# A gated feed-forward block on one core: two more block pairs by seven products, an order of its own for the up projection, and weights laid out as tiles

## The chip, the core and the metric

The kernel runs on one core of one Trainium2 chip. A core has a matrix engine (TensorE, PE in the profile), VectorE (DVE), ScalarE (ACT), GpSimd (POOL) and a sync engine (SP) that issues transfers (DMA). The metric is the device time of one execution in microseconds.

## The reference

One encoder layer on 256 tokens of width D = 2048, in float32, with inputs x, p and the layer's weights:

```python
hn = rmsnorm(x, mix_norm_pre)
z, xbc, dt_raw, u = split(hn @ w_in)
y = concat(ssd_mixer(z, xbc, dt_raw, ...), pool_mixer(u, pool_w, pool_scale))
h = x + rmsnorm(y @ w_out, mix_norm_post)
hn = rmsnorm(h, ffn_norm_pre)
gate, val = split(hn @ w_ffn_up)                      # 2048 -> 2 x 5632
gate = dwconv_centred(gate, ffn_conv_w, ffn_conv_b)   # 3 taps over the tokens, a channel at a time
ff = (gelu(gate) * val) @ w_ffn_down                  # 5632 -> 2048
h = h + rmsnorm(ff, ffn_norm_post)
g = sigmoid(rmsnorm(h, ple_norm_pre) @ w_ple_gate)
out = h + rmsnorm(g * (p @ w_ple), ple_norm_post)
```

Here rmsnorm(v, g) is v divided by the root of its mean square (plus 1e-6) along the channels, times g. `ssd_mixer` is a two-way state-space scan with 16 heads, `pool_mixer` a set of four centred means over windows of 2, 4, 8 and 16 tokens, each followed by a linear map.

## The kernel before

**Numbers in two parts.** Every matmul operand is split into a high part (a cast on ACT to the matmul's reduced float format) and a low part (a subtraction on DVE: the number less its high part). A product takes three matmuls: high by high, high by low and low by high. `split` does that for weights, in pieces of at most 128x1024, into two rings of five buffers each (`whi`, `wlo`); the pieces come from `raw` pages (three buffers of 128x2048), which SP fills by DMA. Further buffers are `page` (13 of 128x2048, for everything long-lived), `mid` (three of 128x1024), `hs` (two of 128x1024, for split hidden values) and eight PSUM banks.

**Stages, in order of time.** The input projection (dtu, xbc, z), the mixers, the output projection (wo), the per-layer embedding's first half (ple0), **up** (11 slabs of 512 hidden channels; each slab has two gate blocks ga and two value blocks va of 64 matmuls), **down** (dn, two halves of 1024 output columns), the second half of the embedding (ple1), the gate (gt), and the end.

**Up.** `feature_pairs` multiplies a block's weights with the normalised input, 16 matmuls for each piece of 128x1024; the norm itself is applied afterwards. `total` adds the two halves of the PSUM result into SBUF (an ACT copy and a DVE add of 128x256, twice for each block). For gates a DVE multiply by the row norm `rfb` follows, then `conv` (three taps for a channel group, on DVE), the gelu on ACT, and once for each slab a 128x1024 DVE multiply by `rfb`, which gives the values their norm (the gelu's result is later multiplied with the values). The product of gelu and values is stored in the six `hid` pages.

**Down.** `token_major` runs over 22 pairs of contraction blocks of 128. A slow pair takes 24 matmuls of 128x512 for a half. A fast pair goes through `seven_products`: a scheme like Strassen's with seven block products for eight, 21 matmuls. It needs sums of weight blocks (`block_sums`, `add_blocks`) and sums of hidden blocks (`pair_sums`, `hid_sums`). `dn_fast` lists the fast pairs, 12 of 22 in either half. The sums of weights for all fast pairs of down and four of gt are made while up runs: `block_sums` fetches a page (dnb, gtb), adds on DVE (L235 to L237) and stores the result to DRAM (dns, gts) through SP; 26 are stored and the last two, for down's first fast pairs, are held in their pages. Sums of hidden blocks are made on DVE (four 128x128 operations, a cast, a 128x512 subtraction) when a pair comes up; four of the twelve are kept in two pages (`dn_keep`) for the second half. `get_hid` casts and subtracts two hidden blocks at a time into an hs buffer.

**What sets the order.** A scheduler of the tile framework orders each engine's instructions by data, by free buffers and by place in the program; it can take work ahead of its place. `tc.issue_after(i)` makes what is issued under it come after instruction i. An engine then works strictly in the order that results. `aside` pops one job of the list `work` after each u step of up. `ready` holds pieces that were split ahead, `at` jobs at a given pair of the second half: `back` (loads the residual h from DRAM into pages hb) at 13 and `first_gate` at 16, which makes the first gate pair's parts from a page gtf, the low part by a copy with negative sign and an accumulating transfer from POOL's queue.

Of the kernel before, what the change touches and what calls it, by code (L numbers as in the profile page):

```python
# [11 lines left out]
F32 = mybir.dt.float32  # L12
F32R = mybir.dt.float32r
AF = mybir.ActivationFunctionType
ALU = mybir.AluOpType

P = 128
# [6 lines left out]
NF = DFF // P  # L24
DPLE = 256
# [26 lines left out]
def build(nc, a, out):  # L52
    x = a["x"][0]
    w_in, w_out, w_up = a["w_in"][0], a["w_out"][0], a["w_ffn_up"][0]
    w_down, w_gate, w_ple = a["w_ffn_down"][0], a["w_ple_gate"][0], a["w_ple"][0]
    out = out[0]

    with tile.TileContext(nc) as tc, \
# [37 lines left out]
        c_dt = DSSD + 1536  # L96
        r0 = wp.tile([P, 2048], F32, tag="raw", bufs=3, name="dtur0")
        for n in range(2):
            first = ins(nc.scalar.dma_start(r0[:, n * 352:(n + 1) * 352],
                                            w_in[:P, c_dt + n * 352:c_dt + (n + 1) * 352]))  # L100
# [55 lines left out]
        def raw(name, src, a_, b_):  # L156
            r = wp.tile([P, 2048], F32, tag="raw", bufs=3, name=name)
            if src is None:
                return r
            last["dma"] = load(r[:, :a_ * b_].rearrange("p (a b) -> p a b", a=a_), src, True)  # L160
            return r
# [33 lines left out]

        def aside():

            for job in (work.pop(0) if work else ()):
                job()
# [8 lines left out]
        def block_sums(name, w, c0, k, held):  # L208


            pg = []

            def fetch():
                r = page(f"{name}b{c0}_{k}")
                pg.append(r)
                load(r.rearrange("p (k c) -> p k c", k=2),
                     w[k * P:(k + 2) * P, c0:c0 + 1024].rearrange("(k p) c -> p k c", p=P))
# [12 lines left out]
            return [fetch], [], [add], [store]  # L230

        def add_blocks(r):

            v = r.rearrange("p (b c) -> p b c", b=4)
            nc.vector.tensor_add(v[:, 0:2], v[:, 0:2], v[:, 1::2])  # L235
            nc.vector.tensor_add(v[:, 3], v[:, 3], v[:, 0])
            nc.vector.tensor_add(v[:, 2], v[:, 2], v[:, 3])  # L237

        def seven_products(name, stage, w, k0, c0, a_, acc, alt, start, stop):
# [3 lines left out]
            if (stage, c0, k0) in sums_:  # L243
                r = raw(f"{name}r", None, 0, 0)
                last["dma"] = load(r[:, 512:1536], w[(k0 + 1) * P:(k0 + 2) * P, c0:c0 + 1024], True)
                last["dma"] = load(r[:, :512], w[k0 * P:(k0 + 1) * P, c0:c0 + 512], True)
# [4 lines left out]
                b11 = split(f"{name}a", r[:, :512], 512)  # L251
                b2 = split(f"{name}b", r[:, 512:1536], 1024)
            else:
                r = t = raw(f"{name}r", w[k0 * P:(k0 + 2) * P, c0:c0 + 1024]
                            .rearrange("(k p) c -> p k c", p=P), 2, 1024)
                b11 = split(f"{name}a", r[:, :512], 512)
                b2 = split(f"{name}b", r[:, 1024:], 1024)
                add_blocks(r)
            t13 = split(f"{name}c", t[:, :1024], 1024)
            t42 = split(f"{name}d", t[:, 1024:], 1024)  # L260
            for x, (wh, wl), c, o, own in (
                    ("a11", b11, 0, alt[0], True), ("a12", b2, 0, acc[0][0], False), ("s4", b2, 512, acc[0][1], False),
                    ("s1", t13, 0, alt[1], True), ("s3", t13, 512, alt[2], True), ("a22", t42, 0, acc[1][0], False),
                    ("s2", t42, 512, alt[3], True)):
# [26 lines left out]
        def token_major(name, w, c0, ks, get, acc, tail=1, fast=(), alt=None, sums=None, at=()):  # L291
# [3 lines left out]
            for u in range(nu):  # L295
# [3 lines left out]
                if u in fast:  # L299
                    if u == fast[0]:  # L300
# [3 lines left out]
                r = None if f"{name}{k0}_0" in ready else raw(f"{name}r{k0}", w[k0 * P:(k0 + 2) * P, c0:c0 + 1024]  # L304
                                                               .rearrange("(k p) c -> p k c", p=P), 2, 1024)
# [8 lines left out]
                for t, (o, c), (k, wh, wl), q in order:  # L314
                    xh, xl = (v[:, t * P:(t + 1) * P] for v in get(k))
                    xx, ww = ((xh, wh), (xh, wl), (xl, wh))[q]
                    mm(o, xx, ww[:, c:c + o.shape[-1]], k == ks[0] and q == 0, k == ks[-1] and q == 2)
# [3 lines left out]
                aside()  # L321

        def feature_major(name, w, c0, get, acc):

            for u in range(4):
                r = raw(f"{name}r{u}", w[u * 512:(u + 1) * 512, c0:c0 + 512]
                        .rearrange("(k p) c -> p k c", p=P), 4, 512)
# [12 lines left out]
        def feature_pairs(name, w, c0, get, acc):  # L340


            for u in range(2):
                r = raw(f"{name}r{u}", w[u * 1024:(u + 1) * 1024, c0:c0 + 256]
                        .rearrange("(k p) c -> p k c", p=P), 8, 256)
                for j in range(2):
                    wh, wl = split(f"{name}{u}_{j}", r[:, j * 1024:(j + 1) * 1024], 1024)
                    for kk in range(4):
                        k = 8 * u + 4 * j + kk
                        for f in range(2):  # L350
                            s = slice(kk * 256 + f * P, kk * 256 + (f + 1) * P)
                            mm(acc[f], wh[:, s], get.both(k), k == 0, False)
                            mm(acc[f][:, L:], wl[:, s], get(k)[0], False, k == NK - 1)
                aside()
# [88 lines left out]
        for u in range(0, NK, 2):  # L443
            r = [wp.tile([P, 2048], F32, tag="raw", bufs=3, name=f"dtur{u}") if u else r0, page(f"dtur{u + 1}")]
            for j in range(2):
                k = u + j
                if k == 0:
                    last["dma"] = load(r[0][:, 704:1056], w_in[:P, c_dt + 704:c_dt + 1056])
# [3 lines left out]
                for c0, c1 in ((0, 704), (704, 1056)) if k == 1 else ((0, 1056),):  # L452
                    last["dma"] = load(r[j][:, c0:c1], w_in[k * P:(k + 1) * P, c_dt + c0:c_dt + c1])
# [29 lines left out]
        with tc.issue_after(half[0]), tc.issue_after(half[1]):  # L483
# [11 lines left out]
            for a_ in range(4):  # L495
# [17 lines left out]
        load(pmat.rearrange("p (g s t) -> p g s t", g=4, s=2),  # L513
             a["pool_matrix"].rearrange("g (s p) t -> p g s t", p=P))
        poolw = page("poolw")
        load(poolw.rearrange("p (g c d) -> p g c d", g=4, c=2),
             a["pool_w"][0].rearrange("g (c p) d -> p g c d", p=P))
# [122 lines left out]
        def xbc(slab):  # L640
            acc = main(f"xbc{slab}")
            feature_major(f"xb{slab}", w_in, DSSD + slab * 512, hn, acc)
# [88 lines left out]
        token_major("z", w_in, 0, list(range(NK)), hn, zacc)  # L731
# [42 lines left out]
        def pair_sums(name, s, o, a11, a21, a12, a22):  # L774

            s1, s2, s3, s4 = (s[:, i * P:(i + 1) * P] for i in range(4))
# [5 lines left out]
            nc.vector.tensor_sub(o[:, 512:], s[:, :512], o[:, :512].bitcast(F32))  # L782
            return {f"s{i + 1}": (o[:, i * P:(i + 1) * P], o[:, 512 + i * P:512 + (i + 1) * P]) for i in range(4)}
# [22 lines left out]
        def sublayer(name, w, ks, get, gain, h, vnext, panel=Panel, fast=((), ()), sums=None, at=()):  # L806
# [3 lines left out]
            for half in range(2):  # L810
# [6 lines left out]
                for t in range(2):  # L817
                    for n in range(2):
# [4 lines left out]
                        nc.scalar.activation(junk, b, AF.Square, accum_out=q)  # L823
                        nc.vector.tensor_mul(mg[t][:, c], b, gain[:, c])
# [40 lines left out]
        dn_fast, gt_fast, dn_keep = ((2, 3, 5, 7, 8, 10, 12, 13, 15, 16, 18, 19), (2, 3, 5, 7, 8, 10, 12, 13, 15, 16, 18, 19)), ((4, 6), (1, 2)), (3, 8, 13, 18)  # L865
# [7 lines left out]
        hid = []  # L873
        for s in range(DFF // 512):
            sc = mid(f"gr{s}")
            for i in range(2):
                ga = main(f"ga{s}{i}")
                feature_pairs(f"ug{s}{i}", w_up, s * 512 + i * 256, hf, ga)
                o = sc[:, i * 512:(i + 1) * 512]
                total(o, ga)  # L880
                v = o.rearrange("p (f t) -> p f t", f=2)
                nc.vector.tensor_tensor(v, v, rfb.unsqueeze(1).to_broadcast([P, 2, L]), op=ALU.mult)
            cv = conv(f"fc{s}", sc, 3, V_FCW + 4 * s, NF, V_FCB + 4 * s)
            nc.scalar.activation(cv, cv, AF.Gelu_apprx_tanh)
            nc.vector.tensor_tensor(cv.rearrange("p (f t) -> p f t", f=4), cv.rearrange("p (f t) -> p f t", f=4),
                                    rfb.unsqueeze(1).to_broadcast([P, 4, L]), op=ALU.mult)
            for i in range(2):
                va = main(f"va{s}{i}")
                feature_pairs(f"uv{s}{i}", w_up, DFF + s * 512 + i * 256, hf, va)
                c0 = (s % 2) * 1024 + i * 512  # L890
                if len(hid) == s // 2:
                    hid.append(page(f"hid{s // 2}"))
                hd = hid[s // 2][:, c0:c0 + 512]
                total(hd, va)
                nc.vector.tensor_mul(hd, hd, cv[:, i * 512:(i + 1) * 512])
# [3 lines left out]
        def get_hid(k):  # L899
            if k % 2 == 0:  # L900
                t = lp.tile([P, 1024], F32R, tag="hs", bufs=2, name=f"hs{k}")
                src = hid[k // 8][:, (k % 8) * L:(k % 8 + 2) * L]
# [187 lines left out]
```

## Time and profile before

| | us |
|---|---|
| median of 3 runs | 1123.46 (1123.09 to 1123.56) |
| the profiled execution's own time | 1123.46 |
| its span, first to last instruction | 1121.6 |
| front: input projection, mixers, output projection (0 to 296) | 296 |
| up, with ple0 ahead of it (296 to 789.1) | 493 |
| down, half 0 and half 1 (789.1 to 1017) | 228 |
| ple1, gate and end (1017 to 1121.6) | 105 |

The granted TensorE clock was 0.999 of full speed on average. In the profile, lines like L87 are lines of the kernel's source; all matmuls are issued from L87 of `mm`, so they are told apart by the names of their result and operands (ga, va for up, dna, dns, dn0s, dn1s for down, gt for the gate). A row of a group has the line, the engine, the operation, out<-in, the shapes, the count, then busy time in us and the mean of one in ns, then idle time of that engine ahead of them and what released it. A row of a timeline or of the chain begins with the start and the duration in us.

### The profile page before, as it was taken

Reading aid. Unit: us, or ns where it says so; the run is one execution under the profiler, and the core shown is the slowest. Engines: PE = TensorE matmul, PEld = TensorE weight load, DVE = VectorE, ACT = ScalarE, POOL = GpSimd, SP = SyncE. Lnnn points to the kernel's source line nnn. Section 1 sums busy time; section 2 is a strip of 40 time slices with the busy share of each in tenths; the row PEclk is TensorE's granted clock in tenths of the full one; section 3 lists DMA queues with packets and bytes.
Section 4 is the critical chain, followed back from the end, with each engine's and each line's share of the span. In section 5 each row is a group of like instructions: output and inputs, shape, how many; then the busy total and the mean of one; then the engine's idle time right before and its main releaser. Section 6 shows DMA issues by size and latency. Waiting matters only on the chain.

```text
span 1121.6 us, 15747 instructions
## 1 busy us (share of the span) xinstructions
PE 1111.2 (99%) x5975; PEld 957.1 (85%) x5975; DVE 928.0 (83%) x1291; ACT 665.4 (59%) x929; POOL 31.1 (3%) x69
## 2 busy tenths in 40 slices
PE   9999999999999999999999999999999999999997
PEld 9999988888888888888888888888888888888876
DVE  6468897799898877877877768878799999899795
ACT  6848663555764554554545545545677777786673
POOL 0200000100100000000000000000000000001001
PEclk9999999999999999999999999999999999999999
DMA  9853447456799989999999898996969688995673
GB/s 361 312 197 104 162 161 277 151 188 189 252 320 349 316 298 340 303 295 313 341 319 310 289 335 303 313 297 218 321 198 336 219 292 295 381 323 175 231 235 107
DMA packets 145996, 300.87 MB, mean 268 GB/s; under 512 B 5504, under 2 KB 98560, under 8 KB 137856
## 3 DMA queue, kind: packets, MB, share of 16 engines
q1 hardware_dynamic: 145216, 298.19, 78.8%
q0 software_dynamic: 272, 1.05, 0.5%
q8 instruction: 47, 0.77, 0.3%
q10 hardware_dynamic: 432, 0.62, 0.2%
q14 instruction: 29, 0.24, 0.1%
HBM read 268.38 MB, written 31.46 MB: 267 GB/s over the span
## 4 chain that ended last, share of the span: by engine, by line
PE 95%; ACT 2%; DVE 1%; issue 1%; DMA 0%; POOL 0%; SPq 0%; POOLq 0%; ACTq 0%
PE va L87 22%; PE ga L87 21%; PE dna L87 14%; PE woa L87 7%; PE xbc L87 6%; PE gt L87 5%; PE z L87 4%; PE dtu L87 4%; PE dns L87 3%; PE dn0s L87 1%; PE dn1s L87 1%; PE ple L87 1%; PE pw L87 1%; PE yd L87 1%; DMA dtur<-w_in 0%
## 5 line engine op out<-in xcount | busy, mean ns | idle before, releaser
L87 PE MATMUL ga<-wox,ug_0h 128*128 128x512 f32 x352 | 125.5, 395 | 0.0
L87 PE MATMUL ga<-wox,ug_1h 128*128 128x512 f32 x352 | 125.1, 394 | 0.0
L87 PE MATMUL va<-wox,uv_1h 128*128 128x512 f32 x352 | 124.8, 393 | 0.0
L87 PE MATMUL va<-wox,uv_0h 128*128 128x512 f32 x352 | 124.8, 393 | 0.0
L87 PE MATMUL ga<-wox,ug_1l 128*128 128x256 f32 x352 | 99.2, 282 | 0.0
L87 PE MATMUL ga<-wox,ug_0l 128*128 128x256 f32 x352 | 99.1, 282 | 0.0
L87 PE MATMUL va<-wox,uv_1l 128*128 128x256 f32 x352 | 99.1, 281 | 0.0
L87 PE MATMUL va<-wox,uv_0l 128*128 128x256 f32 x352 | 99.1, 281 | 0.0
L87 PEld LDWEIGHTS va<-wox,uv_1h 128*128 128x128 f32 x352 | 66.1, 188 | 15.0
L87 PEld LDWEIGHTS va<-wox,uv_0h 128*128 128x128 f32 x352 | 66.1, 188 | 15.0
L87 PEld LDWEIGHTS ga<-wox,ug_0h 128*128 128x128 f32 x352 | 66.1, 188 | 14.9
L87 PEld LDWEIGHTS ga<-wox,ug_1h 128*128 128x128 f32 x352 | 66.1, 188 | 14.9
L87 PEld LDWEIGHTS ga<-wox,ug_0l 128*128 128x128 f32 x352 | 66.2, 188 | 0.1
L87 PEld LDWEIGHTS ga<-wox,ug_1l 128*128 128x128 f32 x352 | 66.2, 188 | 0.0
L87 PEld LDWEIGHTS va<-wox,uv_1l 128*128 128x128 f32 x352 | 66.2, 188 | 0.0
L87 PEld LDWEIGHTS va<-wox,uv_0l 128*128 128x128 f32 x352 | 66.2, 188 | 0.0
L87 PE MATMUL dna<-dn_0h,hs 128*128 128x512 f32 x160 | 50.1, 393 | 0.0
L87 PE MATMUL dna<-dn_1h,hs 128*128 128x512 f32 x160 | 49.9, 393 | 0.0
L235 DVE TENSOR_TENSOR dnb<-dnb 128x1024 f32<-128x1024 f32 x24 | 29.3, 1222 | 14.0 <-DMA dnb<-w_ffn_down 14.0
L903 ACT CAST hs<-hid 128x512 fp32r<-128x512 f32 x44 | 27.1, 617 | 18.3 <-PE dna L87 18.3
L904 DVE TENSOR_TENSOR hs<-hid,hs 128x512 fp32r<-128x512 f32 x44 | 30.2, 686 | 9.1 <-ACT hs L903 9.0
L428 DVE SCALAR_TENSOR_TENSOR fc<-gr,vt,fc 128x255 f32<-128x255 f32 x88 | 36.8, 479 | 0.1
(1909 smaller groups left out, 3060.3 us busy)
## 6 DMA issues: line engine op xcount, KB each, us to landing
dnb<-w_ffn_down SPq DMA_DIRECT2D x24, 1024.0 KB, 10.3
dns<-dnb SPq DMA_DIRECT2D x22, 1024.0 KB, 6.9
dn0r<-w_ffn_down SPq DMA_DIRECT2D x10, 1024.0 KB, 6.2
dn1r<-w_ffn_down SPq DMA_DIRECT2D x10, 1024.0 KB, 6.9
zr<-w_in SPq DMA_DIRECT2D x8, 1024.0 KB, 5.2
dtur<-w_in SPq DMA_DIRECT2D x14, 528.0 KB, 8.5
wo0r<-w_out SPq DMA_DIRECT2D x7, 1024.0 KB, 5.5
wo1r<-w_out SPq DMA_DIRECT2D x6, 1024.0 KB, 5.7
```

The costliest lines, as they stand in the source:

```text
L87: last["pe"] = ins(nc.tensor.matmul(o, lhsT, rhs, start=start, stop=stop, skip_group_check=True))
L235: nc.vector.tensor_add(v[:, 0:2], v[:, 0:2], v[:, 1::2])
L428: nc.vector.scalar_tensor_tensor(o[:, lo:hi], i[:, lo + d:hi + d], vec(wcol + j * wstep + f), o[:, lo:hi], op0=ALU.mult, op1=ALU.add)
L903: nc.scalar.copy(t[:, :512], src)
L904: nc.vector.tensor_sub(t[:, 512:], src, t[:, :512].bitcast(F32))
```

## The change

1. `dn_fast` has 14 of 22 pairs in either half: 2, 3, 4, 5, 7, 8, 9, 11, 12, 13, 15, 16, 18, 19. There are 32 block sums for 28; the last two, for pairs 2 and 3 of half 0, are held.
2. Up has an order of its own. `in_order` chains all ACT, DVE and SP instructions of up, each engine's in program order. `next_part` splits weight pieces five ahead of their matmuls. The jobs of a block sum stand at fixed pieces: fetch at piece 11·i/2 + 2, add and store three pieces later. `add_blocks` makes four adds of 128x512, and the store is issued from POOL instead of SP.
3. Eight sums of hidden blocks (pairs 2, 3, 5, 8, 11, 13, 16, 19) are made during up in an hs buffer, stored to DRAM from POOL, and loaded by POOL in both halves of down into a `mid` buffer. The pages of `dn_keep` are gone.
4. The values go without the norm; the evictions of down get it as a scale instead (ACT's square with scale=row, DVE's scalar-tensor-tensor for the multiply by the gain).
5. The convolution has its three taps on ACT and two adds of 2x255 on DVE, for each gate block.
6. The host lays out the weights as tiles, so that a partition's row of a transfer is contiguous (8 KB for a page). The first-level loads of a fast pair become one transfer of 6 KB a partition.
7. `seven_products` uses its pieces in the order a, b, d, c, with the products a11, a12, a22, s4, s2, s1, s3.
8. The first gate pair is split by ACT and DVE at pair 11 of half 1; ple1's weights are split ahead; the reload of h stands after the last pair; ple0's result is kept in DRAM and loaded back.
9. `get_hid` issues its cast and subtraction after the last ACT and the last DVE instruction of up.

```diff
 def add_blocks(r):
     v = r.rearrange("p (b c) -> p b c", b=4)
-    nc.vector.tensor_add(v[:, 0:2], v[:, 0:2], v[:, 1::2])
-    nc.vector.tensor_add(v[:, 3], v[:, 3], v[:, 0])
-    nc.vector.tensor_add(v[:, 2], v[:, 2], v[:, 3])
+    for i, j in ((1, 0), (0, 3), (3, 1), (2, 3)):
+        nc.vector.tensor_add(v[:, i], v[:, i], v[:, j])
...
 def store():                                   # of block_sums
     if not held:
         t = dp.tile([P, 2048], F32, ...)
-        load(t, pg[0])
+        nc.gpsimd.dma_start(t, pg[0])
...
+def in_order():
+    block = nc.cur_bb.bb.instructions
+    seen = {i.name for i in block}
+    yield
+    for i in block:
+        if i.name in seen or i.engine not in ORDERED:
+            continue
+        if i.engine in chain:
+            tc.add_manual_dep(i, chain[i.engine].name, ..., reason="in_order")
+        chain[i.engine] = i
...
-nc.scalar.activation(junk, b, AF.Square, accum_out=q)
-nc.vector.tensor_mul(mg[t][:, c], b, gain[:, c])
+nc.scalar.activation(junk, b, AF.Square, scale=row[t], accum_out=q)
+nc.vector.scalar_tensor_tensor(mg[t][:, c], b, row[t], gain[:, c], op0=ALU.mult, op1=ALU.mult)
...
+dn_stored = (2, 3, 5, 8, 11, 13, 16, 19)
-work.extend([] for _ in range(8 * DFF // 512))
+jobs_at = [[] for _ in range(NPIECES)]          # NPIECES = 176
 for i, w_ in enumerate(which[2:] + which[:2]):
-    for j, jobs in enumerate(block_sums(*w_, i >= len(which) - 2)):
-        work[3 * i + 2 + j].extend(jobs)
+    fetch, add, store = block_sums(*w_, i >= len(which) - 2)
+    n = 11 * i // 2 + 2
+    jobs_at[n].append(fetch)
+    jobs_at[n + 3].extend((add, store))
...
+for u in dn_stored:
+    jobs_at[16 * (u // 2) + 4 * (u % 2) + 13].extend(hid_sums_jobs(2 * u))
...
+def gate_conv(s, i):
+    v, c, l = (m[:, i * 512:(i + 1) * 512].rearrange("p (f t) -> p f t", f=2) for m in slab[s])
+    for f in range(2):
+        w = V_FCW + 4 * s + 2 * i + f
+        nc.scalar.activation(c[:, f], v[:, f], AF.Identity, bias=vec(...), scale=vec(w + NF))
+        nc.scalar.activation(l[:, f], v[:, f], AF.Copy, scale=vec(w))
+        nc.scalar.activation(v[:, f], v[:, f], AF.Copy, scale=vec(w + 2 * NF))
+    nc.vector.tensor_add(c[:, :, 1:], c[:, :, 1:], l[:, :, :L - 1])
+    nc.vector.tensor_add(c[:, :, :L - 1], c[:, :, :L - 1], v[:, :, 1:])
...
+with in_order():
+    for _ in range(5):
+        next_part()
+    for n in range(NPIECES):
+        s, v, i = blocks[n // 4]
+        if n % 4 == 0:
+            acc = main(f"{'gv'[v]}a{s}{i}")
+        feature_pairs(n % 4, parts[n], hf, acc)
+        if n % 4 == 3:
+            (value_out if v else gate_out)(s, i, acc)
+        next_part()
+        if n >= 4 and n % 4 < 2 and blocks[n // 4 - 1][1] == 0:
+            (gelu if n % 4 else gate_conv)(blocks[n // 4 - 1][0], blocks[n // 4 - 1][2])
+        for job in jobs_at[n]:
+            job()
+ends = [chain[e] for e in ORDERED[:2]]
...
 def get_hid(k):
     if k % 2 == 0:
         t = lp.tile([P, 1024], F32R, tag="hs", bufs=2, name=f"hs{k}")
-        nc.scalar.copy(t[:, :512], src)
-        nc.vector.tensor_sub(t[:, 512:], src, t[:, :512].bitcast(F32))
+        with tc.issue_after(ends[0]), tc.issue_after(ends[1]):
+            nc.scalar.copy(t[:, :512], hid_part(k))
+            nc.vector.tensor_sub(t[:, 512:], hid_part(k), t[:, :512].bitcast(F32))
...
 def hid_sums(k):
     (h1, l1), (h2, l2) = get_hid(k), get_hid(k + 1)
+    o = mid(f"hd{k}", F32R)
+    if k in kept:
+        nc.gpsimd.dma_start(o.bitcast(F32), kept[k])
+        d = sums_in(o)
+    else:
+        d = hid_sums_of(k, sp.tile([P, 512], F32, tag="junk", bufs=1, name=f"hs{k}"), o)
...
-              fast=dn_fast, sums=hid_sums, at={13: back, 16: first_gate})
+              fast=dn_fast, sums=hid_sums, at={11: first, NF // 2: lambda: (ple_parts(), back())}, row=rf)
```

`value_out` and `gate_out` are `total` followed by the multiply with the gelu's result, or with `rfb`.

More of the change, by code (lines that the diff above doesn't have):

```diff
@@ L24 @@
 NF = DFF // P
+NPIECES = DFF // 32
 DPLE = 256
@@ L154, in split, with raw @@
             return hi, lo
-        def raw(name, src, a_, b_):
+        def raw(name, src=None):
             r = wp.tile([P, 2048], F32, tag="raw", bufs=3, name=name)
-            if src is None:
-                return r
-            last["dma"] = load(r[:, :a_ * b_].rearrange("p (a b) -> p a b", a=a_), src, True)
+            if src is not None:
+                last["dma"] = load(r, src, True)
             return r
@@ L338, in feature_major, with feature_pairs @@
                 aside()
[L340 to L354, printed above, removed]
+        def feature_pairs(n, part, get, acc):
+            wh, wl = part
+            for kk in range(4):
+                k = 4 * n + kk
+                for f in range(2):
+                    s = slice(kk * 256 + f * P, kk * 256 + (f + 1) * P)
+                    mm(acc[f], wh[:, s], get.both(k), k == 0, False)
+                    mm(acc[f][:, L:], wl[:, s], get(k)[0], False, k == NK - 1)
         def total(o, acc):
@@ L804, in __call__, with sublayer @@
                             a22=(h2[:, P:], l2[:, P:]))
-        def sublayer(name, w, ks, get, gain, h, vnext, panel=Panel, fast=((), ()), sums=None, at=()):
+        def sublayer(name, w, ks, get, gain, h, vnext, panel=Panel, fast=((), ()), sums=None, at=(), row=None):
             mg = [page(f"{name}m{t}") for t in range(2)]
@@ new lines, in build, with hid_part, hid_sums_of, hid_sums_jobs @@
+            fetch, add, store = block_sums(*w_, i >= len(which) - 2)
+            n = 11 * i // 2 + 2
+            jobs_at[n].append(fetch)
+            jobs_at[n + 3].extend((add, store))
+        hid, kept = [], {}
+        def hid_part(k):
+            return hid[k // 8][:, (k % 8) * L:(k % 8 + 2) * L]
+        def hid_sums_of(k, s, o):
+            return pair_sums(f"he{k}", s, o, *(hid_part(k)[:, i * P:(i + 1) * P] for i in range(4)))
+        def hid_sums_jobs(k):
+            o = []
+            def make():
+                o.append(lp.tile([P, 1024], F32R, tag="hs", bufs=2, name=f"he{k}"))
+                hid_sums_of(k, o[0][:, 512:].bitcast(F32), o[0])
+            def store():
+                kept[k] = dp.tile([P, 1024], F32, tag=f"hsum{k}", bufs=1, name=f"hsum{k}")
+                nc.gpsimd.dma_start(kept[k], o[0].bitcast(F32))
+            return make, store
@@ new lines, in gelu, with value_out @@
+        def gelu(s, i):
+            g = slab[s][1][:, i * 512:(i + 1) * 512]
+            nc.scalar.activation(g, g, AF.Gelu_apprx_tanh)
+        def value_out(s, i, acc):
+            if s % 2 == i == 0:
+                hid.append(page(f"hid{s // 2}"))
+            c0 = (s % 2) * 1024 + i * 512
+            hd = hid[s // 2][:, c0:c0 + 512]
+            total(hd, acc)
+            nc.vector.tensor_mul(hd, hd, slab[s][1][:, i * 512:(i + 1) * 512])
+        with in_order():
+            for _ in range(5):
+                next_part()
+            for n in range(NPIECES):
+                s, v, i = blocks[n // 4]
+                if n % 4 == 0:
[8 more added lines that the diff above has]
+                    job()
```

172 lines of the change are left out of this document (91 added, 81 removed).

## The prediction, made before the changed kernel was run

> **What bounds the kernel now.** First the head of the profile page: its span, the busy time of TensorE, and the chain that ended last, by engine.
>
> ```profile
> span 1121.6 us, 15747 instructions
> ...
> PE 1111.2 (99%) x5975; PEld 957.1 (85%) x5975; DVE 928.0 (83%) x1291; ACT 665.4 (59%) x929; POOL 31.1 (3%) x69
> ...
> PE 95%; ACT 2%; DVE 1%; issue 1%; DMA 0%; POOL 0%; SPq 0%; POOLq 0%; ACTq 0%
> ```
>
> TensorE (PE) is idle for 1121.6 − 1111.2 = 10.4 us. Whatever does not remove matmuls can win at most that. Next the windows by stage tell where those 10.4 us are, and the chain of waits gives the pace.
>
> ```profile
> core 0: us, PE busy (x) PEld busy (x) DVE busy (x) ACT busy (x) POOL busy (x), PEclk, DMA share, GB/s
> 0.00:53.00 53.00, 51.45 (x308) 50.38 (x308) 28.61 (x40) 40.61 (x56) 7.07 (x16) 1.00 0.95 356
> ...
> 320.00:789.00 469.00, 469.00 (x2690) 411.66 (x2689) 377.71 (x490) 235.72 (x311) 0.00 (x0) 1.00 0.94 308
> 789.00:903.00 114.00, 114.00 (x496) 92.64 (x496) 105.59 (x147) 82.17 (x109) 0.00 (x0) 1.00 0.76 259
> 903.00:1017.00 114.00, 113.95 (x494) 92.29 (x493) 104.97 (x143) 84.39 (x109) 3.35 (x8) 1.00 0.92 325
> ...
> 1110.00:1122.00 12.00, 4.57 (x26) 2.91 (x24) 3.95 (x8) 3.05 (x10) 1.63 (x4) 0.85 0.34 112
> ```
>
> ```profile
> 766.78 22.33 PE va L87 x128
> 789.10 11.11 PE dna L87 x48
> ...
> 809.89 5.55 PE dna L87 x24
> ```
>
> Up (320 to 789) has no PE idle time, and the two halves of down (789 to 1017) have 0.05 us; 12.0 − 4.57 = 7.4 of the 10.4 us lie in the last 12 us, and 53.00 − 51.45 = 1.6 at the start. The last up block ends at 766.78 + 22.33 = 789.11, and the first down matmul starts at 789.10: the border has no gap. In down one 128x512 matmul costs 5.55 / 24 = 0.2313 us.
>
> **The matmuls that go.** A slow pair of contraction blocks takes 24 matmuls in a half, a fast one 21. Two more fast pairs in each half remove 2 x 2 x 3 = 12, and at 0.2313 us that is −2.78 us. As a check of the pace: before, a half has 10 x 24 + 12 x 21 = 492 matmuls, 113.8 us at that pace, and the windows show 114.
>
> **What hides, and is costed at nothing.** Host tiles make long rows of each weight transfer, the multiply of the values by the norm leaves VectorE (DVE) in up, and the convolution taps move from DVE to ScalarE (ACT).
>
> ```profile
> DMA packets 145996, 300.87 MB, mean 268 GB/s; under 512 B 5504, under 2 KB 98560, under 8 KB 137856
> ...
> L428 DVE SCALAR_TENSOR_TENSOR fc<-gr,vt,fc 128x255 f32<-128x255 f32 x84 | 35.2, 479 | 0.1
> ...
> L885 DVE TENSOR_TENSOR fc<-fc,rfb 128x1024 f32<-128x1024 f32 x11 | 13.5, 1225 | 0.3 <-ACT fc L884 0.2
> ```
>
> Two thirds of the packets are under 2 KB, and the DMA engines are 94% busy in up; yet PE waits for none of it there (469.00 of 469). DVE is rid of 13.5 us and of most of 35.2 us, in a stage where it has 469 − 378 = 91 us to spare; ACT, which gets the taps, has 233. All of this is worth 0; its cover is the full PE row, and it can cost something only if an engine or the DMA becomes later than PE. Bounds: no gain in up; at the start at most the 1.6 us of idle time, of which I take nothing because those loads keep their row length.
>
> The last step of each down half gets the norm as a scale. Eight DVE operations become scalar-tensor-tensor. The nearest row is L428, 479 ns for 255 elements; two of those for 512 elements are 0.96 us, where the present multiply is one of the 0.69 us operations below. At most 8 x 0.27 = 2.2 us on DVE, half of it beside the next half's matmuls: 0 to 1.1, I take 0.
>
> **The border from up to down.** This is the step that decides. Before, the casts of the first hidden pairs (hs) were made long ahead of down:
>
> ```profile
> L903 ACT CAST hs<-hid x3: 610/622/622, 334.9 to 794.7; 128x512 fp32r<-128x512 f32 x3
> ```
>
> That row answers for the hs tile from 320 to 800: the first of the three starts at 334.9, 454 us ahead of use. In the changed kernel `get_hid` issues them after `ends`, the last ACT and the last DVE instruction of up. So the engine orders are these. ACT: both copies of the last block's values, between them one cast of a weight piece, then the cast for hs0, for which PE's first down matmul waits. DVE: the last value adds, the product with the gate (`value_out`), then four `add_blocks` operations of 128x512 for the last block sum (job at n = 175 of 176 pieces), mixed with one 128x512 and one 128x128 operation of the hidden sums of pair 4, and only then the subtraction for hs0. PE has eight matmuls that need only the high part; the ninth waits for that subtraction. The timelines of ACT and DVE at the border show the instructions that stay, and a busy stretch of DVE gives the pace:
>
> ```profile
> 788.79 0.37 ACT L359 COPY hid<-va 128x256 f32<-128x256 f32 x1 [1.44 <-PE va L87]
> 789.07 0.62 ACT L152 CAST dn04ah<-dn04r 128x512 fp32r<-128x512 f32 x1
> 789.59 0.37 ACT L359 COPY hid<-va 128x256 f32<-128x256 f32 x1
> ```
>
> ```profile
> 789.72 0.69 DVE L153 TENSOR_TENSOR dn04al<-dn04r,dn04ah 128x512 fp32r<-128x512 f32 x1
> 790.33 0.41 DVE L360 TENSOR_TENSOR hid<-hid,va 128x256 f32<-128x256 f32 x1
> 790.78 0.69 DVE L895 TENSOR_TENSOR hid<-hid,fc 128x512 f32<-128x512 f32 x1
> ```
>
> ```profile
> 805.93 0.69 DVE L904 TENSOR_TENSOR hs<-hid,hs 128x512 fp32r<-128x512 f32 x1
> 806.53 1.22 DVE L153 TENSOR_TENSOR dn_0l<-dn0r,dn_0h 128x1024 fp32r<-128x1024 f32 x1
> 807.66 1.22 DVE L153 TENSOR_TENSOR dn_1l<-dn0r,dn_1h 128x1024 fp32r<-128x1024 f32 x1
> 808.80 0.68 DVE L153 TENSOR_TENSOR dn010al<-dn010r,dn010ah 128x512 fp32r<-128x512 f32 x1
> 809.40 0.69 DVE L782 TENSOR_TENSOR he<-hd,he 128x512 fp32r<-128x512 f32 x1
> ...
> 812.88 0.29 DVE L777 TENSOR_TENSOR hd<-hid 128x128 f32<-128x128 f32 x1
> 813.08 0.29 DVE L778 TENSOR_TENSOR hd<-hid 128x128 f32<-128x128 f32 x1
> ```
>
> From start to start, a 128x512 operation takes 809.40 − 808.80 = 0.60 us, a 128x1024 one 807.66 − 806.53 = 1.13, a 128x128 one 0.20. The hs0 cast follows the second copy as the cast at 789.07 follows the first, 0.28 later: 789.87 + 0.62 = 790.49. First stall: 790.49 − 789.10 = 1.4 us. Eight matmuls, 8 x 0.2313 = 1.85, end at 792.34. On DVE the gate product starts at 790.78, the next operation 0.60 later, then 5 x 0.60 + 0.20 = 3.20: the hs0 subtraction starts at 794.58 and ends 0.69 later, at 795.27. Second stall: 795.27 − 792.34 = 2.9 us. Together +4.3 us. Behind the waiting matmuls nothing else of PE can run, since it is in order. The lower bound is the first stall alone, 1.4, if the adds do not stand in the way. The upper one comes from the transfer of that last block sum (dnb):
>
> ```profile
> dnb<-w_ffn_down SPq DMA_DIRECT2D x24, 1024.0 KB, 10.3
> ...
> DMA to landing us min/median/max: 4.5/8.7/13.3
> ```
>
> SP issues it after the split of the last up piece has begun, which needs the slot of piece 170: 789.1 − 5 pieces x 2.79 (22.33 / 8) = 775.2, and a cast and a subtraction later about 777.5. It lands at 787.8 by the 10.3 of the first row, at 790.8 by the maximum of the tile's row; DVE asks for it at 791.4. Two us later would make the stall 6 us.
>
> **Inside down.** With start-to-start values a fast pair costs DVE 0.60 + 3 x 1.13 for its pieces and 0.60 for hs = 4.6 us, and 4 x 0.20 + 0.60 = 1.4 more where the hidden sums are not stored, 6.0; a slow pair 2 x 1.13 + 0.60 = 2.9. PE needs 21 x 0.2313 = 4.86 and 5.55. Pairs 7, 8, 9 run in a row, and 7 and 9 are not stored: DVE needs 16.6, PE 14.6, so DVE falls back 2.0 us, where before no run was longer than two (6.0 + 4.6 − 9.7 = 0.9, hidden, by the full PE row). In half 1 the split of the first gate pair, 2 x 1.13, also falls between 10 and 11. The rings carry a lead of about a pair's piece, 1 to 2.5 us, so I take +1.0 for both halves, from 0 to 3.
>
> **Sum** against the profiled run (1123.46, equal to the median of the runs; 1.9 lie outside its span): 1123.46 − 2.78 + 4.3 + 1.0 = 1126.0. Its own range is 1123.1 (1.4 at the border and 1.0 inside) to 1129.7 (6 and 3). About 0.2%, 2.25 us, is what a measurement of this kernel can tell from no change.
>
> **Rivals.** (A) The border is cheap: hs0's subtraction gets in front of the adds, or DVE is early because up has unburdened it, so that only the cast's 1.4 us or nothing is paid, and down hides its excess as before. For it: DVE's lighter up stage. Against it: the adds stand before the subtraction, and the gate product just before them waits for the last matmul, so no lead helps. Time: 1123.46 − 2.78 + 0 to 1.4 = 1120.7 to 1122.1. It decides if hs0's low part is there by 792.
>
> (B) Transfers from POOL's queue are late. The block sums and 16 loads of 0.5 MB of stored hidden sums (hd) move there. Before, one 1 MB transfer went that way:
>
> ```profile
> L949 POOL DMA_DIRECT2D gtfl<-w_ple_gate x1: 1426/1426/1426, 980.8 to 980.8; - x1
> ...
> DMA to landing us min/median/max: 14.4/14.4/14.4
> ```
>
> `mid` has three buffers, so a load can begin when the pair three fast pairs back is done; for pair 5 that is 2 x 4.86 us ahead, for pair 11 4.86 + 5.55, and in each the sums are first used after 9 matmuls, 2.1 us: leads of 11.8 and 12.5, and 17 or more for the others. At 14.4 us these are late by 2.6 and 1.9, in both halves: +9 us, 1135.0. It decides from 11.8 us on. Against it: half the bytes, and long rows where that one had short; stores have 22 us (eight pieces) before their page is wanted. [...]
>
> (C) Down becomes bound by DVE: the excess of the unstored runs is paid in full (2.0 at 7 to 9, 0.8 at 11 to 13, 0.6 at 2 to 5, each twice, and 2.3 for the gate pair) = 9.1 instead of 1.0, so up to 1134; half of that paid is 1129.6. DMA at 92% in half 1 pushes the same way. Against it: slow pairs give back 2.7 us each.
>
> (D) The long rows speed up the start and the front: at most 1.6 us there, so 1124.4 with the border stall; with a cheap border, 1119.1.
>
> **How the numbers follow.** Forecast 0.47, A 0.25, B 0.08, C 0.13, D 0.07. Faster (below 1121.2): most of A and a part of D, 0.20. Same: the rest of A, D and the lowest part of the forecast's range, 0.27. Slower: 0.53. Range 1120.9 to 1130.5: it takes in most of A, all of the forecast and half of C, and leaves out B and the ends.
>
> **What would show it.** After: twelve matmuls fewer than 5975, give or take missing records; va blocks at 22.33 each 128; a gap of 1.4 us ahead of the first dna and of 2.9 us after eight of them, released by ACT and DVE hs; hid sums landing from POOL in under 11.8 us; PE idle of 1 us over down. I am wrong if the first 24 dna matmuls take 5.55 us from the end of va, if waits for hd or for weight pieces take over 3 us in down, or if up shows gaps.

## The result and the profile after

The changed kernel takes 1125.91 us (median; 1124.09 to 1126.89 without one run of 1366.02 us, whose mean granted clock was 0.752), the kernel before 1123.16 beside it: a ratio of 1.0021, 95% interval 1.0015 to 1.0028. It is slower by 2.75 us. The profiled execution took 1124.48 us, 1.4 less than the median; that difference turns out to have a cause of its own.

The head of the profile page of the changed kernel, for comparison with the same lines of before:

```profile
span 1122.7 us, 15935 instructions
...
PE 1107.8 (99%) x5963; PEld 954.8 (85%) x5963; DVE 933.8 (83%) x1293; ACT 713.9 (64%) x1036; POOL 63.8 (6%) x122
...
PE 95%; DVE 2%; ACT 2%; DMA 1%; issue 1%; POOL 0%; POOLq 0%; ACTq 0%
```

Twelve matmuls fewer (5975 to 5963) and 3.4 us less of busy PE, in a span that is 1.1 us longer: PE idles 4.5 us more. The windows by stage of the changed kernel show where:

```profile
core 0: us, PE busy (x) PEld busy (x) DVE busy (x) ACT busy (x) POOL busy (x), PEclk, DMA share, GB/s
320.00:789.00 469.00, 468.76 (x2687) 411.22 (x2685) 383.82 (x509) 279.27 (x413) 21.61 (x40) 1.00 0.88 341
789.00:795.00 6.00, 2.10 (x8) 1.42 (x8) 5.83 (x12) 2.28 (x5) 0.00 (x0) 1.00 0.93 339
795.00:903.00 108.00, 107.88 (x468) 87.75 (x469) 97.46 (x123) 81.12 (x99) 4.32 (x8) 1.00 0.81 300
903.00:1017.00 114.00, 114.00 (x496) 92.79 (x495) 109.24 (x141) 86.96 (x114) 8.47 (x11) 1.00 0.94 358
```

Up and both halves of down are full, as before. In the six microseconds from 789 to 795 PE is busy for 2.10. PE's timeline there, and the chain of waits through it:

```profile
788.48 0.28 PE L90 MATMUL va<-wox,uv_1l 128*128 128x256 f32 x1
790.24 0.70 PE L90 MATMUL dna<-dn_0h,hs 128*128 128x512 f32 x2 [1.47 <-issue]
...
795.12 1.20 PE L90 MATMUL dna<-dn_0h,hs 128*128 128x512 f32 x4 [2.79 <-DVE hs L990]
```

```profile
790.44 0.04 DVE hid L964
...
791.05 0.70 DVE dnb L253
...
791.77 0.69 DVE dnb L253
792.46 0.60 DVE hd L792
793.06 0.60 DVE dnb L253
793.66 0.20 DVE hs L787
793.87 0.60 DVE dnb L253
794.47 0.61 DVE hs L990
...
795.12 9.52 PE dna L90 x40
```

The chain leaves PE and runs on DVE: the product with the gate, four adds of the last block sum with two operations of the hidden sums between them, then hs0's subtraction, and only then PE again. Of the first stall the row says "issue", since the wait names nothing; PE restarts where the first of the two hs casts ends. The timelines of ACT and DVE have these casts and subtractions in rows of two:

```profile
789.51 1.15 ACT L989 CAST hs<-hid 128x512 fp32r<-128x512 f32 x2
```

```profile
794.38 1.28 DVE L990 TENSOR_TENSOR hs<-hid,hs 128x512 fp32r<-128x512 f32 x2
```

By starts against the pace of the matmuls the gaps are 1.63 and 2.96 us, 4.6 together (the idle times in the rows, 1.47 and 2.79, are shorter, because a matmul's row reaches past the start of the next one: a row of 0.39 us at 788.25, the next start at 788.48).

### The profile page after: what moved, and what is told of

Same layout as the page of the kernel before. It is cut to its first block, busy times and chain, and to the rows that moved or that the text cites. A ratio compares the mean times of both kernels' runs of the same rounds, so it can differ in the third digit from the quotient of the medians.

```text
span 1122.7 us, 15935 instructions
## 1 busy us (share of the span) xinstructions
PE 1107.8 (99%) x5963; PEld 954.8 (85%) x5963; DVE 933.8 (83%) x1293; ACT 713.9 (64%) x1036; POOL 63.8 (6%) x122
## 3 DMA queue, kind: packets, MB, share of 16 engines
q0 software_dynamic: 7776, 44.04, 10.7%
## 4 chain that ended last, share of the span: by engine, by line
PE 95%; DVE 2%; ACT 2%; DMA 1%; issue 1%; POOL 0%; POOLq 0%; ACTq 0%
PE va L90 22%; PE ga L90 21%; PE dna L90 13%; PE woa L90 7%; PE xbc L90 6%; PE gt L90 5%; PE z L90 4%; PE dtu L90 4%; PE dns L90 3%; PE dn1s L90 2%; PE dn0s L90 2%; PE ple L90 1%; DMA dtur<-w_dtu 1%; PE pw L90 1%; PE yd L90 1%
## 5 line engine op out<-in xcount | busy, mean ns | idle before, releaser
L253 DVE TENSOR_TENSOR dnb<-dnb 128x512 f32<-128x512 f32 x112 | 77.3, 690 | 2.7
L90 PE MATMUL dna<-dn_0h,hs 128*128 128x512 f32 x128 | 40.8, 394 | 4.3 <-DVE hs L990 2.8
L90 PE MATMUL dna<-dn_1h,hs 128*128 128x512 f32 x128 | 40.6, 393 | 0.0
L244 POOL DMA_DIRECT2D dns<-dnb x26 | 14.1, 543 | 333.7 <-DVE dnb L253 304.8
```

The source lines that it names most:

```text
L90: last["pe"] = ins(nc.tensor.matmul(o, lhsT, rhs, start=start, stop=stop, skip_group_check=True))
L244: nc.gpsimd.dma_start(t, pg[0])
L253: nc.vector.tensor_add(v[:, i], v[:, i], v[:, j])
```

## The experiments

**The changed kernel again, and the clock.**

> The changed kernel once more, beside the next three. Its profiled run took 1124.48 us; from the two traces -2.78 (matmuls), +4.6 (two stalls at the border from up to down: 1.63 and 2.96) and -0.35 (start) make 1123.46 + 1.4 less rounding = 1124.5 to 1124.9. But the median of its runs is 1125.9, with granted clocks of 0.995 to 0.998 where before had 0.999. Theory T1: the 1.4 us that the trace does not show are a lower granted clock in most runs, so runs of about 1124.3 go with a clock of 0.998 and those of 1126 with 0.996. Rival T2: they are a stall or a transfer that the profiled run happened not to have; then runs of 1126 have the same clock and a gap in the trace.

It measured 1125.96 us (1123.93 to 1127.27, 11 runs; ratio 1.0022, 1.0013 to 1.0031), and this time the profile fell on a run of 1126.04 us. Its gaps are those of the first profile, 1.64 and 2.95. What differs shows in the windows of one microsecond behind the second gap; the third column from the right is the granted clock. First this run, then the same stretch of the run of 1124.48:

```profile
793.00:794.00 1.00, 0.00 (x0) 0.00 (x0) 1.00 (x4) 0.00 (x0) 0.00 (x0) 1.00 1.01 426
...
796.00:797.00 1.00, 1.00 (x4) 0.81 (x3) 0.36 (x2) 0.42 (x1) 0.00 (x0) 0.50 0.99 418
797.00:798.00 1.00, 1.00 (x4) 0.71 (x4) 0.34 (x1) 0.63 (x1) 0.00 (x0) 0.50 1.03 434
798.00:799.00 1.00, 1.00 (x4) 0.80 (x3) 0.89 (x1) 0.00 (x0) 0.00 (x0) 0.50 1.03 434
799.00:800.00 1.00, 1.00 (x5) 0.80 (x4) 0.00 (x0) 0.00 (x0) 0.00 (x0) 0.81 0.69 213
800.00:801.00 1.00, 1.00 (x6) 0.80 (x5) 0.00 (x0) 0.00 (x0) 0.00 (x0) 1.00 0.57 209
```

```profile
796.00:797.00 1.00, 1.00 (x6) 0.82 (x5) 0.36 (x2) 0.59 (x1) 0.00 (x0) 1.00 0.99 418
```

From about 796.0 to 799.4 PE runs at half its clock, four matmuls a microsecond started instead of six, and no row names a wait. Half of 3.4 us is 1.7, as an estimate of the loss; from the first matmul of down to the first of gt this run needs 236.2 us, the other 234.6, so 1.6 more. T1 holds and T2 falls. The runs split in two groups: 4 of 11 here, and 5 of 18 of the first series, lie at 1123.9 to 1124.5, the others at 1125.4 to 1127.3. The mean clocks on record go with them: 0.998 in all nine of the shorter runs, 0.995 to 0.997 in all twenty of the longer ones. Why only part of the runs is hit, no run shows.

**The first hidden pairs cast inside up.**

```diff
+        jobs_at[169].append(early_hid(0))   # cast and subtraction of hs0
+        jobs_at[171].append(early_hid(2))   # of hs2
...
 def get_hid(k):
-    if k % 2 == 0:
+    if k % 2 == 0 and k in early_hs:
+        cur["t"] = early_hs.pop(k)
+    elif k % 2 == 0:
...
```

> The casts and subtractions of the first two hidden pairs (hs0, hs2) are made inside up, at pieces 169 and 171 of 176, instead of after its last ACT and DVE instruction. Theory S (the border stall is 4.6 us and nothing replaces it): 1125.9 - 4.6 = 1121.3, so under the kernel before (1123.2) by 1.9. Rival R1 (the backlog on DVE only moves the wait to the first fast pair): 1123 to 1125.5, with a gap before the matmuls of pair 2 about 11 us after the border. On the clock: if the stall's restart is what lowers it, it returns to 0.999 and the time is 1123.2 - 2.8 - 0.3 = 1120.1; if not, it stays near 0.996 and the time is 1121.3.

1119.66 us (1119.25 to 1119.93, 7 runs), ratio 0.9969 (0.9958 to 0.9981): 6.3 us under the changed kernel and 3.4 under the kernel before. PE's timeline at the border, and the windows of down:

```profile
788.62 0.28 PE L90 MATMUL va<-wox,uv_1l 128*128 128x256 f32 x1
788.74 0.62 PE L90 MATMUL dna<-dn_0h,hs 128*128 128x512 f32 x2
```

```profile
789.00:903.00 114.00, 114.00 (x496) 92.84 (x495) 105.99 (x137) 86.47 (x111) 4.30 (x8) 1.00 0.84 311
903.00:1017.00 114.00, 114.00 (x500) 92.87 (x499) 109.32 (x141) 86.25 (x111) 9.97 (x16) 1.00 0.93 361
```

No gap at the border, none at pair 2 (R1 falls), none in either half. The gain is 4.6 of stalls and 1.7 of the clock behind them; 1120.1, the value for "the restart lowers it", was the nearer one, and the clock is 1.00 in both halves. The mean clock of the runs did not return to the 0.999 expected (0.997 to 0.998, as for the kernel before beside it): it also counts the last microseconds of the kernel, where PE has little to do and the clock is lowered (in the profile of the changed kernel 0.83 from 1110 to 1123, with PE busy for 5.53 of 13 us). Of the 3.4 us, 2.78 are matmuls; where the rest comes from was not singled out.

**Only the adds moved.** One edit, `n = 11 * i // 2 + 2` becomes `n = 16 * i // 3 + 2`.

> The block sums are spaced 16/3 pieces apart instead of 11/2, so that the adds of the last one stand five pieces earlier, before the last value block. hs0 stays behind the last instruction of up. Theory S: the first stall (ACT's cast, 1.6 us) stays, the second (DVE's subtraction behind four adds, 2.96 us) goes to 0 to 0.3: 1125.9 - 2.8 = 1123.1. If the adds are not the cause of the second stall (rival: the subtraction waits for the cast or the gate product alone), it stays: 1125.9.

1121.39 us (1121.10 to 1121.63, 11 runs), 4.6 under the changed kernel. The second gap is gone and the first stays; PE's timeline:

```profile
790.08 0.70 PE L90 MATMUL dna<-dn_0h,hs 128*128 128x512 f32 x2 [1.47 <-issue]
...
792.01 1.09 PE L90 MATMUL dna<-dn_0h,hs 128*128 128x512 f32 x4
```

The stall went as expected. The time fell by 1.6 more than the stall's 2.96, the price of the lowered clock (1.00 from 789 to 800 here), and no run of the eleven shows a second group. The first stall by itself is the difference to the kernel above, 1.73 us by medians, 1.63 in the trace.

**One add moved.** The last block sum is fetched three pieces earlier and its first add made two pieces earlier.

> The changed kernel with the first of the four adds of the last block sum moved ahead (its fetch too), so that three adds and one 128x512 subtraction of the hidden sums stand before hs0's subtraction. First gap 1.63 as before; second gap 790.44 + 5 x 0.6 + 0.69 - 792.16 = about 2.0, where it was 2.96 (clock lowered to 0.50 for 3 us after it in most runs) and 2.40 with 12 pairs (lowered too), and none was lowered after a gap of 1.63. Without a lowered clock: 1121.4 + 2.0 = 1123.4 in every run; with it, runs at 1123.4 and others at 1125. Rival (the lowered clock has nothing to do with the gap): part of the runs 1.6 us longer whatever the gap.

1124.22 us (1123.29 to 1125.74, 11 runs): six runs at 1123.3 to 1124.2, five at 1125.1 to 1125.7. The second gap is 2.17, and the profile (of one of the longer runs) has the clock at 0.50 behind it. So behind a gap of 2.2 us the clock fell in part of the runs, by their times 5 of 11 here against 20 of 29 at 2.96, and behind one of 1.63 in none of 11.

**Twelve fast pairs, with the stall and without it.** Pairs 4 and 9 go back to 24 matmuls; n = 11·(i + 4)/2 + 2 keeps the end of the sums in place.

> The changed kernel with 12 fast pairs in each half instead of 14 (pairs 4 and 9 go back to 24 matmuls), the block sums ending at the same piece. Theory S: 12 matmuls more, 2.78 us: 1125.9 + 2.8 = 1128.7, and the border stall as before at 4.6. Rival R2 (fourteen pairs already cost part of their gain inside down, by DVE or DMA): less than +2.8, down to +1.

1127.75 us (1126.55 to 1129.18, 5 runs): +1.8, less than 2.8, but not by R2: the gap at the border was 2.40 instead of 2.96 here, and five runs of two groups make a poor median. Their two lowest are 2.3 over the shorter group of the changed kernel, where 2.78 − 0.56 = 2.2 would be due. So the same was done without the stall:

> The kernel with hs0 and hs2 made inside up (1119.7) and 12 fast pairs in each half instead of 14, block sums ending at the same piece. No stall and no lowered clock at the border in either, so the difference is down alone. Theory: 12 matmuls of 0.2313 us, 1119.7 + 2.8 = 1122.4. Rival (fourteen pairs cost part of their gain inside down): 1120.7 to 1122.

1122.36 us (1122.04 to 1122.75, 11 runs): +2.70 for twelve matmuls, against 2.78. R2 falls. With twelve fast pairs, as many as before, and no stall, this kernel is 0.7 us under the kernel before (1123.04 beside it): so much of the 3.4 comes from other parts of the change, and no run shows from which.

**Why fourteen pairs cost nothing inside down.**

```diff
-        dn_stored = (2, 3, 5, 8, 11, 13, 16, 19)
+        dn_stored = ()                        # on top of hs0, hs2 inside up
```

> The kernel with hs0 and hs2 made inside up (1119.7), without stored sums of hidden blocks: all fourteen fast pairs of each half make them on DVE as they come up, and POOL's sixteen loads of 0.5 MB are gone. Theory F (the stored sums are what lets down take fourteen pairs without a stall): DVE gets 8 x 1.4 = 11 us more in each half, 109.3 + 11 = 120 of the 112 us that PE needs, so at least 8 us more in half 1 and 3 or more in half 0: 1128 to 1136. Rival: the sums are hidden either way, 1119.7, or less if POOL's loads cost something.

1127.71 us (1127.37 to 1128.27, 5 runs), +8.05: just under the range of theory F. The windows of down show DVE at its end:

```profile
789.00:903.00 114.00, 113.44 (x491) 91.26 (x490) 111.98 (x168) 86.77 (x114) 0.46 (x2) 1.00 0.72 266
903.00:1017.00 114.00, 110.80 (x469) 86.51 (x467) 113.28 (x173) 85.57 (x113) 0.00 (x0) 1.00 0.85 320
```

**The kernel before with fourteen pairs.** Its `dn_fast` gets the new list, its jobs `work[5 * i // 2 + 2 + j]`.

> The kernel before with one edit: 14 fast pairs in each half, the same list as in the change, and the jobs of the 32 block sums 2.5 instead of 3 steps apart. Everything else as before: DVE with the taps and the values' norm, four hidden sums kept in pages, stores on SP, short rows. Theory S (only the matmuls count): 1123.1 - 2.8 = 1120.3. Rival (the other parts are needed to feed fourteen pairs): DVE needs 6.0 us for an unstored fast pair where PE takes 4.86, ten of fourteen unstored: 14 x 4.6 + 10 x 1.4 + 8 x 2.9 = 101.6 of 112.4 us in a half, locally short, so 1121 to 1126 with stalls on dn pieces or hidden sums in down, or on wider DMA use in up.

1135.21 us (1134.46 to 1136.23, 4 runs), ratio 1.0109: 12 us slower, by the rival and beyond it. Up ends 5.4 us later than before, down takes 7.6 more. The window of up, and what PE waited for:

```profile
320.00:789.00 469.00, 466.00 (x2655) 407.61 (x2654) 380.45 (x495) 228.16 (x307) 0.00 (x0) 1.00 0.95 324
```

```profile
PE dns L87 <- ACT dn026ch L152: 3.7, 1, 3.7
...
PE ga L87 <- DVE ug_0l L153: 1.3, 2, 0.8
PE va L87 <- ACT uv_0h L152: 0.9, 1, 0.9
```

In up it is the splits of weights that come late, and not their transfers: the page for the piece wanted at 594.5 (uv60r) was issued by 577.0 and its loads landed 8.0 us after their issue in the median, but its cast started at 594.40, on ACT behind a gelu that waited for the taps on DVE, and these stood behind an add of a block sum. In down one piece stands on ACT behind casts that wait for hidden sums on DVE. In the half with the gap of 3.9 us (3.7 in the waits) the mean clock is 0.99, where the kernel before has 1.00. Behind two gaps in up with a few matmuls between them (0.90 and 0.79 us in the waits) the clock is 0.70 from 595 to 600 and 0.96 from 600 to 605.

**Which other parts carry that?** Three runs, each on top of hs0 and hs2 inside up (1119.66).

The outer taps go back to DVE: in `gate_conv` two `scalar_tensor_tensor` for each f replace the two ACT operations and the two adds.

> The kernel with hs0 and hs2 made inside up, with the two outer taps of the convolution back on DVE (88 scalar-tensor-tensor operations of 255, 479 ns each, for 44 adds of 2x255) and off ACT. Theory: DVE has 84 of 469 us to spare in up, the operations take about 12 us more: no change, 1119.7 within 0.5. Rival: in the fixed order DVE's pieces come later and up gets gaps: above 1121.

1119.62 us (1119.39 to 1120.33, 7 runs): no change. In the window of up DVE has 392.0 of 469 us instead of 385.1, and PE is full.

The up weights get short rows:

```diff
-"w_up": tiles(a["w_ffn_up"][0], 8, 256).reshape(2, DFF // 512, 2, 2, P, 2048),
+"w_up": ....reshape(2, DFF // 512, 2, 2, 8, P, 256),   # loaded with "k p c -> p k c"
```

> The kernel with hs0 and hs2 made inside up, with the up weights alone in DRAM so that a transfer has rows of 1 KB instead of 8 KB, as before the change. Theory H (long rows are needed for the bytes of 14 pairs): up moves 341 GB/s at 88% busy with long rows; 92 MB of its 160 MB in short rows at 325 GB/s make 96% or more busy, and weights come late at times: 1121 to 1127, with gaps in up like those of the kernel before with 14 pairs (6.6 us). Rival (DMA is hidden anyway): 1119.7.

1119.70 us (1119.50 to 1120.36, 7 runs): no change, and theory H falls. Packets and the window of up of this kernel:

```profile
DMA packets 129758, 326.05 MB, mean 292 GB/s; under 512 B 5648, under 2 KB 96656, under 8 KB 107536
```

```profile
320.00:789.00 469.00, 469.00 (x2689) 411.67 (x2688) 385.56 (x511) 281.30 (x417) 21.61 (x40) 1.00 0.98 343
```

The DMA engines are 98% busy and bring 343 GB/s, more than in the kernel before with fourteen pairs (95%, 324 GB/s), and PE waits for none of it. So it was the order of the splits that up lacked there, and not speed of the transfers. Which part of the new order mends it (the chain, or pieces split five ahead) was not separated.

The stores of the block sums go back to SP, `load(t, pg[0])` for `nc.gpsimd.dma_start(t, pg[0])`:

> The kernel with hs0 and hs2 made inside up, with the stores of the block sums issued from SP instead of POOL. Theory G (POOL's queue matters since SP must not wait): a store stands on SP until its adds are done, which come 8 pieces after SP has got there; the weight loads behind it are then issued 4 pieces (11 us) later, land about 7 us after their split was due, and the split has 8.8 us of slack: from no change to 2 us for some of the 30 stores, 1119.7 to 1130. Rival: POOL's transfers themselves cost something (late stores hold the pages), then faster than 1119.7.

1315.58 us (1313.71 to 1316.86, 4 runs), far outside both. What SP's queue and PE waited for:

```profile
SPq L120 <- DVE dnb L253: 202.6, 18, 14.0
SPq L120 <- DMA dnb<-w_down: 187.7, 26, 9.1
```

```profile
PE va L90 <- ACT uv_0h L153: 68.9, 16, 8.9
PE ga L90 <- ACT ug_0h L153: 52.4, 14, 7.9
```

The mechanism is theory G's, its size was far off: SP stands up to 14 us on a store's adds, with the loads of weights behind it, and the gaps come at most sums. In up's fixed order the stores must not be on the queue that fetches weights.

The clock is lowered at these gaps too, to 0.89 on average from 320 to 789. In the gap of 5.61 us that ends at 352.73 it falls: the five windows of two microseconds from 350 to 360 have 0.81, 0.50, 0.50, 0.50 and 0.98, which makes 6.8 us at 0.50, from about 351.2 to 358.1. Where other runs' windows show both ends of such a stretch it is half as long: summed in the same way, 3.41 us for the changed kernel (the run of 1126.04), 3.41 with twelve fast pairs, 3.42 with one add moved and 3.4 in up of the kernel before with fourteen pairs. The length of a gap alone does not tell whether the clock falls: the two profiles of the changed kernel have the same gaps (1.63 and 2.96, 1.64 and 2.95), and the clock falls behind the second in the run of 1126.04 and not in the run of 1124.48. What else decides it was not shown.

**Fifteen pairs.** Pairs 2 to 6, 8 to 11, 13 to 16, 18 and 19, the sums 5.1 pieces apart, on top of hs0 and hs2 inside up.

> The kernel with hs0 and hs2 made inside up, and 15 fast pairs in each half (2 to 6, 8 to 11, 13 to 16, 18, 19), 34 block sums 5.1 pieces apart. If DVE and DMA still keep up: 6 matmuls less, 1119.7 - 1.4 = 1118.3. Rival: DVE, busy 109.3 of 114 us in half 1 at 14 pairs, cannot: a fast pair in place of a slow one asks 1.7 to 3.1 us more of DVE in each half and takes 0.7 us from PE's time, 112 of 113; then stalls of several us in down: 1120 to 1125.

1122.77 us (1121.26 to 1123.47, 11 runs), 3.1 slower than with fourteen. There is one gap of 2.16 us, in half 1, and a lowered clock in that half (0.99; half 0 has 1.00). With 1.39 us of matmuls less, and 1.7 for the clock, this makes 2.5 of the 3.1. The runs form two groups again: four at 1121.3 to 1121.9 with mean clocks of 0.998 and 0.999, seven at 1122.5 to 1123.5 with 0.997. The waits of PE:

```profile
PE dna L90 <- ACT dn122dh L153: 2.0, 1, 2.0
```

The cast that PE waits for stands on ACT behind a cast of hidden sums, for which ACT waited 3.62 us for DVE. One list of fifteen was tried, with the same eight stored sums; of the lists tried fourteen pairs is the most that pays. The fastest kernel of the case is the one with hs0 and hs2 inside up.

## Why the prediction was right, and where it was not

The forecast of 1126.0 met 1125.91, but through misses that cancel, and that the two agree to 0.1 us is luck. The border, the step that it called decisive, was right in mechanism and size. With what the runs gave for each term the sum is 1123.16 − 2.70 (matmuls) − 0.7 (the rest of the change) + 4.6 (border) + 1.6 (clock) = 1126.0.

- **The matmuls**: −2.78 forecast, 2.70 measured between 12 and 14 pairs without a stall.
- **What hides**: right for what was tried. Taps on ACT (1119.62 without) and long rows of the up weights (1119.70 without) are worth nothing in the kernel of 1119.66. The values' norm was not tried alone. Some part costed at nothing is worth the 0.7 that twelve pairs without the stall show; which one stays open. At the start nothing was won: PE is busy for 51.3 of the first 53 us, 51.5 before.
- **The border**: stalls of 1.4 and 2.9 forecast, 1.63 and 2.96 in the trace. hs0's subtraction, forecast to start at 794.58, started at 794.38 in DVE's timeline, behind the same instructions. The transfer of the last block sum was not late: DVE went on to its adds without a pause.
- **What failed: inside down, +1.0.** It is 0; both halves are full with fourteen pairs. The step set DVE's excess of 2.0 us in a run of three against too short a lead. In the kernel of 1119.66 DVE has 105.99 and 109.32 of 114 us and makes hidden sums ahead: in half 0 those of pairs 7 and 9 are done at 812.3 and 825.1, while the run of pairs 7, 8 and 9 has its matmuls from 824.8 on and first needs the sums of pair 9 at 836.5. Only without the stored sums (+8.05) or with a fifteenth pair (one gap) does the excess come to light.
- **What was missing: the clock.** The sum priced each stall at its length. The second costs 1.6 to 1.7 us more in two of three runs (20 of 29), and moves the median by about that. It took the place of the 1.0, and with the 0.3 by which the border was set too low it made up for the 0.7 as well.

The rivals: (A) a cheap border did not come about; where hs0 and hs2 were moved ahead of the adds by an edit, the time was 1119.66, below its 1120.7 to 1122.1. (B) POOL's transfers are not late. The rows of its loads and stores, and the landing times of the loads:

```profile
dns<-dnb POOLq DMA_DIRECT2D x26, 1024.0 KB, 5.1
...
hd<-hsum POOLq DMA_DIRECT2D x16, 512.0 KB, 7.4
```

```profile
DMA to landing us min/median/max: 4.3/7.4/10.7
```

At most 10.7 us for the loads, under the 11.8 from which they would count, and the stores, with 5.1, beat the 6.9 they took from SP before. The one accumulating transfer of 14.4 us was a poor guide. (C) shows only without the stored sums, (D) not at all. The price of (C) was a little high: by the step's own values the runs at 11 to 13 and 2 to 5 fall back by 0.6 and 0.3 us, not 0.8 and 0.6, so it comes to about 8 and not 9.1.

## What to carry to other kernels

At a border between two stages, look at what stands on each engine ahead of the first operand of the next stage: a fence such as "after the last instruction of the stage before" puts it behind every background job there, and moving two small casts ahead was worth more than twelve matmuls (6.3 us against 2.7). Price a stall of PE with the lowered clock that can follow it: here it cost about 1.6 us more in part of the runs with a gap of 2.16 to 2.96 us, and two gaps of 0.90 and 0.79 close together had it behind them too. Expect two groups of run times then; one profiled run may show the cheaper one (1124.48 beside a median of 1125.91). A change that removes work pays only together with what feeds it: the same fourteen pairs cost 12 us in the old arrangement, where splits of weights stood behind other work.

## What the runs showed of the hardware

- Behind gaps of 2.95, 2.40 and 2.17 us the granted clock of PE was 0.50 for 3.4 us in the profiled runs (3.41, 3.41 and 3.42), with one of 2.16 its mean over half 1 was 0.99. The cost was 1.6 us (236.2 against 234.6 us in the two profiles of the changed kernel). By the two groups of times it came in 20 of 29 runs at 2.96, in 3 of 5 at 2.40, in 5 of 11 at 2.17, in 7 of 11 at 2.16 and in none of 11 at 1.63. Only the profiled runs show where the clock fell; the others are counted by their times, and their mean clocks agree.
- The length of a gap did not settle it: with the same gaps, to 0.01 us, the clock fell to 0.50 in the run of 1126.04 and stayed at 1.00 in the run of 1124.48. With the stores on SP it stayed at 0.50 for 6.8 us around the end of a gap of 5.61.
- With the up weights in rows of 1 KB the DMA engines were 98% busy at 343 GB/s over 469 us, with POOL's stores among them, without a wait of PE.
